# Attention issued as a listed order of small steps on three engines, and two moves in the rounds of an S5 stage

## The chip, the cores and the metric

The kernel runs on one core of a Trainium2 chip. The metric is the device time of that core in microseconds, as the median of several runs. Before the change it is 1025.93 us, the median of 3 runs from 1025.42 to 1026.64. Engines are named as the profile names them: PE is TensorE (matrix products and transposes, with PEld for its weight loads), DVE is VectorE, ACT is ScalarE, POOL is GpSimd, and SP is the engine that issues the large transfers.

## What is computed

A decoder trunk of two layers over one sequence of 256 tokens with 1024 channels in float32. Each layer is half a SwiGLU block, a mixer, and half a SwiGLU block again. Layer 0 mixes with S5, a diagonal state-space recurrence; behind it one set of keys and values is made. Layer 1 mixes with attention of three branches (compressed, selected, window) over that set. Cut to what matters here:

```python
def _swiglu(x, w_in, w_out):                 # D_FF 2816
    a, b = jnp.split(x @ w_in, 2, axis=-1)
    return (jax.nn.silu(a) * b) @ w_out

def _s5_mixer(u, ..., w_glu):                # 64 groups of 16 channels, 64 states
    bu_re = jnp.einsum('bsgh,gph->bsgp', ug, bb_re)      # and bu_im
    _, _, x_re, x_im = lax.associative_scan(combine, (la_re, la_im, bu_re, bu_im), axis=1)
    y = einsum(x_re, c_re) - einsum(x_im, c_im) + d_skip * ug
    y = jax.nn.gelu(y.reshape(bsz, seq, D_MODEL))
    return y * jax.nn.sigmoid(y @ w_glu)

def _nsa_mixer(u, kv, w_qg, q_norm, w_o, rel_bias):      # 16 heads in 4 groups, head size 64
    qg = u @ w_qg
    q = _rmsnorm(qg[..., :1024].reshape(bsz, seq, 4, 4, 64), q_norm)
    gates = jax.nn.sigmoid(qg[..., 1024:].reshape(bsz, seq, 4, 4, 3))
    o = gates[..., 0:1] * o_cmp + gates[..., 1:2] * o_slc + gates[..., 2:3] * o_win
    return o.reshape(bsz, seq, D_MODEL) @ w_o

for layer in range(2):
    h = h + 0.5 * _swiglu(_rmsnorm(h, ffn1_norm[layer]), ...)
    h = h + mixer(_rmsnorm(h, mix_norm[layer]))
    h = h + 0.5 * _swiglu(_rmsnorm(h, ffn2_norm[layer]), ...)
```

## The kernel before

**Products and weights.** A float32 product is made of three products of a shorter type. Each operand is split into a high part and a remainder, and `mm3` (lines 139 to 141) adds high times high, remainder times high and high times remainder in one bank. Weights come as raw blocks of 1 MB over SP's queue into two buffers. ACT copies the high part (`whi`, lines 92, 105, 131) and DVE subtracts it for the remainder (`wlo`, lines 96, 108, 132); there are five buffers for each. The left operand, the normalised activations `xT`, is made by PE transposes (line 180) that ACT and DVE empty in the same two parts (lines 188 and 189, or 164 and 165). An object `Acts` does that for one half of a token tile at a time (`fill`). After the first of tile 1 has been filled it also issues the squares of all rows (line 156, ACT) and the reciprocal root of their means (`rs`, lines 160 and 161, DVE and POOL).

**The blocks.** A SwiGLU block takes its weights from a generator of split blocks and multiplies chunk after chunk. At its end it hands each finished half of a token tile to `done`, which fills the operand of what follows. PE has no gap between the blocks if that operand and the first split weights are there.

**S5** works in eight rounds `cb` of 8 groups. PE makes the drive of the states (`dr`, line 542), DVE rotates it (`turn_in`, line 522), scans (line 559) and rotates back (`turn_out`, with POOL adding up `z`, line 566), and PE makes the outputs (`yb`, lines 573 and 580), which ACT passes through the gelu. The GLU product of the round before (`ga`, lines 139 to 141) lies between, and each round also splits the weights of the round three later (`weights`, lines 92 and 96). Here DVE, ACT and PE run in the order in which the program is written (`manual_schedule`), so the order of the calls in the loop is the order in each engine's queue. Ahead of the rounds stand 15 products whose result nothing reads (line 612). A round in short, with the two neighbours that matter below:

```python
turn_out(cb)
if cb + 3 < KT:
    weights(cb + 3)          # high part on ACT, remainder on DVE
outputs(cb)
if cb + 1 < KT:
    turn_in(cb + 1, dr)
```

**Attention** is cut into about 35 units in a string `ORD`: `q` makes the queries of one of four head groups ("chunks") for both token tiles, `t` transposes them, `l` makes the logits and exponentials of one group and one token tile, `c` the compressed branch of a group, `m` scales the exponentials, transposes them and multiplies by the values, `p` adds a part of the final projection. The string gives priorities to the compiler's scheduler, which orders the single instructions of neighbouring units on each engine. In `queries` the two token tiles go together: both are scaled (`qs`, line 875) and squared (line 878) by ACT, one DVE call sums the squares of both, POOL raises them to the power -1/2 (`hrr`, line 715), one DVE call multiplies (line 885), and the two are split and transposed (line 894) into `qT`. The first chunk is 304 columns wide, since it also has the gates (line 877); the others have 256. Logits (`s`, line 930) go to two banks, with two more (`x`) for the window part of token tile 1; DVE adds the bias and finds the maximum (lines 936 and 938), ACT takes the exponential (line 941). The projection's last part adds to `h` and calls `done`, which fills the operand of the last SwiGLU block.

Engines take their queues strictly in order, and an instruction that waits holds all behind it.

## Time and profile before

| | us | PE busy us | granted clock |
|---|---|---|---|
| median of 3 runs | 1025.93 | | |
| profiled execution | 1024.85 | | |
| its span, first to last instruction | 1023.1 | 984.84 | 0.988 |
| 0 to 219: first SwiGLU block | 219.00 | 209.56 | 1.00 |
| 219 to 330: most of S5 | 111.00 | 104.29 | 0.92 |
| 330 to 711.7: end of S5, two SwiGLU blocks, keys and values | 381.70 | 378.73 | 1.00 |
| 711.7 to 833.4: attention | 121.70 | 106.59 | 0.97 |
| 833.4 to 1023: last SwiGLU block | 189.60 | 185.67 | 1.00 |

The span is the time from the first to the last instruction of one profiled execution. Times within it count from its first instruction. The granted clock is the share of PE's full speed that it was allowed; a matrix product takes twice as long at 0.50. A stage in which PE is busy for its whole length at clock 1.00 can only become shorter if PE gets less to do.

### The profile page before, as it was taken

What the parts mean: (1) busy time and instruction counts of PE and PEld (TensorE: products, weight loads), DVE (VectorE), ACT (ScalarE), POOL (GpSimd) and SP (SyncE); (2) the same over time, 40 slices, a digit from 0 to 9 for tenths busy, and PEclk for the clock granted to TensorE, in tenths of its full rate; (3) what the DMA queues carried; (4) which work ended last, traced back from release to release, by engine and by line L of the source; (5) the groups of instructions that cost most, each with busy time, mean ns of one, the idle gap of its engine ahead of it and who ended that gap; (6) DMA issues with size and microseconds to landing.
All of it is one profiled execution on the core that took longest, in us unless ns stands there. A gap on an engine that the chain in (4) does not pass through costs nothing.

```text
span 1023.1 us, 14326 instructions
## 1 busy us (share of the span) xinstructions
PE 984.8 (96%) x5532; PEld 802.5 (78%) x5532; DVE 658.8 (64%) x1194; ACT 578.9 (57%) x1015; POOL 80.1 (8%) x88
## 2 busy tenths in 40 slices
PE   6999999989999999999999999999798899999998
PEld 5888887778778877888878888888676678888886
DVE  4999954479765455567565555556588866655553
ACT  5677675544465345456655555554687665555552
POOL 3001120313110000000032000000200000000000
PEclk9999999979999999999999999999899999999999
DMA  7556564443157657664645455553511145555642
GB/s 264 184 191 212 196 206 130 159 121 109 63 175 206 181 164 202 210 225 149 248 160 201 132 202 174 197 185 106 170 31 54 42 148 195 193 190 181 204 171 78
DMA packets 28948, 168.96 MB, mean 165 GB/s; under 512 B 4560, under 2 KB 7184, under 8 KB 10064
## 3 DMA queue, kind: packets, MB, share of 16 engines
q1 hardware_dynamic: 28656, 167.26, 49.0%
q8 instruction: 43, 0.70, 0.3%
q0 software_dynamic: 224, 0.79, 0.2%
q14 instruction: 25, 0.20, 0.1%
HBM read 165.54 MB, written 2.49 MB: 164 GB/s over the span
## 4 chain that ended last, share of the span: by engine, by line
PE 88%; DVE 4%; ACT 4%; POOL 1%; issue 1%; DMA 0%; SPq 0%; ACTq 0%; POOLq 0%
PE mm L139 17%; PE mm L140 16%; PE mm L141 16%; PE o L140 8%; PE o L141 8%; PE o L139 8%; PE tr L226 2%; PE dr L542 1%; PE x L969 1%; PE tr L959 1%; PE ga L141 1%; PE tr L797 1%; ACT Pt L941 1%; PE tr L180 1%; PE ga L139 1%
## 5 line engine op out<-in xcount | busy, mean ns | idle before, releaser
L139 PE MATMUL mm<-whi,xT 128*128 128x512 f32 (+2 forms) x800 | 313.9, 394 | 9.8 <-ACT qst L878 4.0
L141 PE MATMUL mm<-whi,xT 128*128 128x512 f32 (+2 forms) x800 | 307.3, 385 | 1.4 <-DVE xT L189 1.4
L140 PE MATMUL mm<-wlo,xT 128*128 128x512 f32 (+2 forms) x800 | 307.5, 385 | 0.6 <-DVE wlo L96 0.5
L108 DVE SCALAR_TENSOR_TENSOR wlo<-raw,gains,whi 128x512 fp32r<-128x512 f32 x288 | 203.6, 748 | 94.1 <-ACT whi L105 90.9
L105 ACT ACTIVATE whi<-raw,gains 128x512 fp32r<-128x512 f32 x288 | 192.1, 718 | 115.1 <-PE mm L141 51.1
L96 DVE TENSOR_TENSOR wlo<-raw,whi 128x1024 fp32r<-128x1024 f32 x148 | 182.1, 1236 | 109.6 <-ACT whi L92 109.2
L92 ACT ACTIVATE whi<-raw 128x1024 fp32r<-128x1024 f32 x148 | 155.0, 1059 | 123.9 <-PE mm L141 48.4
L139 PEld LDWEIGHTS mm<-whi,xT 128*128 128x128 f32 x800 | 151.9, 190 | 41.1 <-ACT qst L878 4.5
L141 PEld LDWEIGHTS mm<-whi,xT 128*128 128x128 f32 x800 | 151.6, 190 | 31.5 <-DVE xT L189 1.9
L140 PEld LDWEIGHTS mm<-wlo,xT 128*128 128x128 f32 x800 | 152.3, 190 | 28.4 <-DVE wlo L96 1.5
L140 PE MATMUL o<-wlo,turned 128*128 128x512 f32 x352 | 137.8, 391 | 0.1
L141 PE MATMUL o<-whi,turned 128*128 128x512 f32 x352 | 137.5, 391 | 0.0
L139 PE MATMUL o<-whi,turned 128*128 128x512 f32 x352 | 137.1, 392 | 0.0
L140 PEld LDWEIGHTS o<-wlo,turned 128*128 128x128 f32 x352 | 66.1, 188 | 14.3 <-DVE wlo L96 1.0
L141 PEld LDWEIGHTS o<-whi,turned 128*128 128x128 f32 x352 | 66.2, 188 | 13.6
L139 PEld LDWEIGHTS o<-whi,turned 128*128 128x128 f32 x352 | 66.0, 188 | 13.8 <-ACT g L265 0.3
L265 ACT ACTIVATE g<-mm,rs 128x256 f32<-128x256 f32 x88 | 41.0, 471 | 44.5 <-PE mm L141 44.0
L266 DVE SCALAR_TENSOR_TENSOR g<-mm,rs,g 128x256 f32<-128x256 f32 x88 | 41.8, 482 | 36.9 <-ACT g L265 36.8
L165 DVE TENSOR_TENSOR turned<-tr,turned 128x512 fp32r<-128x512 f32 x44 | 30.3, 689 | 31.9 <-ACT turned L164 31.6
L164 ACT ACTIVATE turned<-tr 128x512 fp32r<-128x512 f32 x44 | 26.2, 595 | 38.7 <-PE tr L226 38.6
L941 ACT ACTIVATE Pt<-Pt,mx 128x128 f32<-128x128 f32 (+1 forms) x64 | 28.4, 447 | 4.4 <-DVE mx L936 4.3
L161 POOL TENSOR_TENSOR rs<-ms,nhalf 128x1 f32<-128x1 f32 x12 | 6.6, 554 | 302.3 <-DVE ms L160 302.3
(298 smaller groups left out, 941.4 us busy)
## 6 DMA issues: line engine op xcount, KB each, us to landing
raw<-in_w_in_dram SPq DMA_DIRECT2D x87, 1024.0 KB, 4.9
raw<-in_w_out_dram SPq DMA_DIRECT2D x44, 1024.0 KB, 4.9
raw<-in_w_kv_dram SPq DMA_DIRECT2D x6, 1024.0 KB, 4.8
raw<-in_w_glu_dram SPq DMA_DIRECT2D x4, 1024.0 KB, 4.9
raw<-in_w_o_dram SPq DMA_DIRECT2D x4, 1024.0 KB, 4.9
raw<-in_w_qg_dram SPq DMA_DIRECT2D x6, 512.0 KB, 3.6
B<-revd SPq DMA_DIRECT2D x8, 256.0 KB, 7.9
raw<-in_w_qg_dram SPq DMA_DIRECT2D x2, 608.0 KB, 3.8
```

The source lines that it names most:

```text
L92: Last.act = S.activation(hi, r, AF.Copy)
L96: Last.dve = V.tensor_tensor(out=lo, in0=r, in1=hi.bitcast(F32), op=ALU.subtract)
L105: Last.act = S.activation(hi[:, c], r[:, c], AF.Identity, scale=g_)
L108: i = V.scalar_tensor_tensor(out=lo[:, c], in0=r[:, c], scalar=g_, in1=hi[:, c].bitcast(F32), op0=ALU.mult, op1=ALU.subtract)
L139: T.matmul(ps, lhsT=xh, rhs=wh, start=start, stop=False)
L140: T.matmul(ps, lhsT=xh, rhs=wl, start=False, stop=False)
L141: Last.pe = T.matmul(ps, lhsT=xl, rhs=wh, start=False, stop=stop_)
L164: i = S.activation(dst_hi, src, AF.Copy)
L165: V.tensor_tensor(out=dst_lo, in0=src, in1=dst_hi.bitcast(F32), op=ALU.subtract)
L265: Last.act = S.activation(sl, acc[t][:, 0:256], AF.Silu, scale=rs[:, t:t + 1])
L266: Last.dve = V.scalar_tensor_tensor(out=g[:, t, :], in0=acc[t][:, 256:512], scalar=rs[:, t:t + 1], in1=sl, op0=ALU.mult, op1=ALU.mult)
L941: S.activation(Pt[:, r, br], Pt[:, r, br], AF.Exp, scale=-1.0, bias=mx[:, c:c + 1], accum_out=sm[:, c:c + 1])
```

## The change

The change has three parts.

1. **Attention.** `ORD` and its units are replaced by `ORDER`, a list of 397 names, and the scheduler is switched off for PE, ACT and DVE, so that the list is the order in each queue. A name is a letter with numbers: `h w` split the query weights, `g` makes six products of a query chunk for one token tile, `a b n i j y x` are the norm, split and transposes of one chunk and one token tile, `l v e` the logits, bias and exponential of one head, `c C k K q z Z` the compressed branch, `s S` the scaling, `t T P` the transposes, their copies and the product with the values, `o O` the split of the output, `D H W M` the weights and products of the projection, `A B Y U` the addition to `h` and the operand of the last block. The norm of the queries is now by token tile, each with its own squares, sums, power and multiply. The norm factor and the operand of token tile 1 are made in attention (`f F J Q R`), while tile 0's are made at the end of the block before (`fill_half`). `E` is an exponential of one element whose result nothing reads. `L N V` load and split the first weights of the last SwiGLU block (the class `Ahead`).
2. **S5, round zero.** Ten products whose result nothing reads are issued ahead of `turn_out(0)`.
3. **S5, all rounds.** `weights` is cut in two: the high part stays where it was, the remainder on DVE goes behind `turn_in(cb + 1)`.

The code, cut; the steps that are left out hold the old units' instructions, one or two to a step:

```diff
+        def norm(self):
+            for u in range(4):
+                row_square(self.h, u // 2, u % 2, self.ss)
+            for u in range(2):
+                row_rstd(u, self.ss, self.rs)
+
+        def fill(self, t, kq, norm=True):
+            pv = self.turn(t, kq)
...
+            if norm and t + kq == 2:
...
+    class Ahead:
...
+        def load(self):
+            n = len(self.raws)
+            self.raws.append(load_granule(self.w_in[n // 2, n % 2], 512))
+
...
+            def weights(k, part):
+
+                r = raws[k // 2][:, (k % 2) * 1024:(k % 2 + 1) * 1024]
+                if part == 0:
+                    hi, lo = hip.tile([P, 1024], F32R, name="whi"), lop.tile([P, 1024], F32R, name="wlo")
+                    S.activation(hi, r, AF.Copy)
+                    gw[k] = [(hi[:, n * 512:(n + 1) * 512], lo[:, n * 512:(n + 1) * 512]) for n in range(2)]
+                    rooms[k] = hi, lo
+                    return
+                hi, lo = rooms.pop(k)
+                V.tensor_tensor(out=lo, in0=r, in1=hi.bitcast(F32), op=ALU.subtract)
                 if k in (2, 3):
                     raws.append(load_granule(A["w_glu"][k], 512))
+
...
+            def spin(ps, n):
+
+                for i in range(n):
+                    T.matmul(ps, lhsT=gw[0][0][0][:, 0:P], rhs=gw[0][0][0], start=True, stop=True)
...
+                    if cb == 0:
+                        spin(gacc[1][1], 10)
                     turn_out(cb)
                     if cb + 3 < KT:
-                        weights(cb + 3)
+                        weights(cb + 3, 0)
                     outputs(cb)
                     if cb + 1 < KT:
                         turn_in(cb + 1, dr)
+                    if cb + 3 < KT:
+                        weights(cb + 3, 1)
                 for t in range(2):
                     yk[t, 0] = y_tokens(t, 0, pd, "dr")
...
-    ORD = "q0 q1 t0 l00 l01 q2 t1 c0 m00 l10 m01 l11 q3 t2 c1 m10 l20 m11 l21 t3 c2 m20 l30 m21 l31 c3 p0 p2 m30 p4 m31 p6"
...
+    ORDER = """
+    Q0 f0 d10 g000 F00 f1 g001 J00 d11 F01 h100 F10 J01 w100 d20 F11 g010 J10 g002 h110 J11 Q1 g011 g003 g012 R g013 a00 w110 b00
+    a01 d21 g110 b01 h200 n00 g111 w200 g100 g112 g101 E i00 j00 g113 h210 y00 x00 g102 n01 d30 w210 l000 i01 j01 l001 a11 v000 y01
...
+    def attention(x, hc, ahead):
...
+            def step_g(n, t, i):
+                if i == 0:
+                    qa[n, t] = mm_bank()
+                w = width(n)
+                for k in (2 * i, 2 * i + 1):
+                    u = (n, k // 4, 0 if n else k % 4 // 2)
+                    c = (k % 4 if n else k % 2) * w
+                    mm3(qa[n, t][:, 0:w], xT, k, t, (wh[u][:, c:c + w], wl[u][:, c:c + w]), k == 0, k == KT - 1)
...
+            def step_a(n, t):
+                q, v = tp.tile([P, 256], F32, name="qs"), tp.tile([P, 4, 2, 64], F32R, name="qst")
+                qq[n, t], qv[n, t] = q, v
+                    S.activation(rsh[:, t:t + 1], rs[:, t:t + 1], AF.Copy, scale=0.5)
+                S.activation(v.rearrange("p h a d -> p (h a d)")[:, 0:256].bitcast(F32), qa[n, t][:, 0:256], AF.Square, scale=rs[:, t:t + 1])
+                S.activation(q, qa[n, t][:, 0:256], AF.Identity, scale=rs[:, t:t + 1])
+                if n == 0:
+                    S.activation(gate[:, t].rearrange("p h b -> p (h b)"), qa[n, t][:, 256:304], AF.Tanh, scale=rsh[:, t:t + 1])
+
+            def step_E():
+                S.activation(small.tile([P, 1], F32, name="warm"), rsh[:, 1:2], AF.Exp)
+
+            def step_b(n, t):
+                ss, ms = tp.tile([P, 4], F32, name="hss"), tp.tile([P, 4], F32, name="hms")
+                sq = qv[n, t].rearrange("p h a d -> p (h a d)")[:, 0:256].bitcast(F32)
+                V.tensor_reduce(out=ss, in_=sq.rearrange("p (h d) -> p h d", d=64), axis=mybir.AxisListType.X, op=ALU.add)
+                V.tensor_scalar(out=ms, in0=ss, scalar1=1.0, scalar2=64 * EPS, op0=ALU.mult, op1=ALU.add)
+                rr = tp.tile([P, 4], F32, name="hrr")
+                G.tensor_tensor(out=rr, in0=ms, in1=nhalf[:, 0:4], op=ALU.pow)
+                qp[n, t] = rr
...
+            def step_n(n, t):
+                q3 = qq[n, t].rearrange("p (h d) -> p h d", d=64)
+                V.tensor_tensor(out=q3, in0=q3, in1=qp[n, t].unsqueeze(2).to_broadcast([P, 4, 64]), op=ALU.mult)
...
+            def step_l(g, t, r):
+                ps = s_bank()
+                parts = [(ps[:, 0:400], 0, 400)] if t == 0 else [(ps[:, 0:KWN], 0, KWN), (x_bank()[:, 0:256], KWN, KW)]
+                for i in range(2):
+                    for p_, c0, c1 in parts:
+                        T.matmul(p_, lhsT=qT[:, g * 4 + r, t * P:(t + 1) * P], rhs=KV.kT[:, i, g, c0:c1], start=i == 0, stop=i == 1)
+                lb[g, t, r] = ps, ps[:, KWN:400] if t == 0 else parts[1][0]
...
+            def step_T(g, t, kb, br):
+                pts[g, t, kb, br] = pt_room[:, turn[0] % 4]
+                turn[0] += 1
+                if br:
+                    V.tensor_copy(pts[g, t, kb, br], tp_[g, t, kb, br])
+                else:
+                    S.activation(pts[g, t, kb, br], tp_[g, t, kb, br], AF.Copy)
...
+            steps = {k[5:]: f for k, f in locals().items() if k.startswith("step_")}
+            for kh in range(2):
+                step_d(0, kh)
+                for j in range(2):
+                    step_h(0, kh, j)
+                    step_w(0, kh, j)
+            with tc.manual_schedule(engines={V.engine, S.engine, T.engine}):
+                for u in ORDER.split():
+                    steps[u[0]](*(int(i) for i in u[1:]))
+            Nxt.x.norm()
...
+    def fill_half(hc, gain):
+
+        def done(t, hf):
+            if t == 0 and hf == 0:
+                acts(hc, gain)
+            if t == 0:
+                Nxt.x.fill(0, hf, norm=False)
+                row_square(hc, 0, hf, Nxt.x.ss)
+                if hf:
+                    row_rstd(0, Nxt.x.ss, Nxt.x.rs)
         return done
...
-        ffn(x, 3, A["w_in1_1"], A["w_out1_1"], h, bg=bg, steps=1, done=fill_next(h, 4))
-    attention(Nxt.x, h, fill_next(h))
+        ffn(x, in_granules(A["w_in1_1"], 3), A["w_out1_1"], h, bg=bg, steps=1, done=fill_half(h, 4))
+    ahead = Ahead(A["w_in2_1"], 5)
+    attention(Nxt.x, h, ahead)
...
-    ffn(Nxt.x, 5, A["w_in2_1"], A["w_out2_1"], h, done=store)
+    ffn(Nxt.x, ahead, A["w_out2_1"], h, done=store)
```

How this moves instructions is shown at three places, one row for each instruction in an engine's queue: line, operation, what is written and what is read, size; numbers behind a name tell buffers apart.

The first place is ACT's queue where the first query products end, before the change (`h` is squared into `ss`, `mm` are the query banks, `qst` holds the queries' squares and later their split, `whi` are high parts of weights):

```order
L156 ACTIVATE junk_6156,ss_6082<-h_75 128x512
L156 ACTIVATE junk_6158,ss_6082<-h_75 128x512
L156 ACTIVATE junk_6160,ss_6082<-h_75 128x512
L875 ACTIVATE qs_6268<-mm_6198,rs_6081 128x256
L156 ACTIVATE junk_6162,ss_6082<-h_75 128x512
L131 ACTIVATE whi_6493<-raw_6491 128x1024
L877 ACTIVATE gate_6193<-mm_6198,rsh_6188 128x48
L878 ACTIVATE qst_6269<-mm_6198,rs_6081 128x256
L875 ACTIVATE qs_6268<-mm_6199,rs_6081 128x256
L877 ACTIVATE gate_6193<-mm_6199,rsh_6188 128x48
L878 ACTIVATE qst_6269<-mm_6199,rs_6081 128x256
```

Four squares of rows for both token tiles, one of them and a weight split within the evacuations of the two banks, stand here. The same place after the change, from the first evacuation on:

```order
L1003 ACTIVATE qst_6292<-mm_6205,rs_6091 128x256
L1004 ACTIVATE qs_6291<-mm_6205,rs_6091 128x256
L1006 ACTIVATE gate_6169<-mm_6205,rsh_6165 128x48
L1002 ACTIVATE rsh_6165<-rs_6091 128x1
L1003 ACTIVATE qst_6306<-mm_6243,rs_6091 128x256
L1004 ACTIVATE qs_6305<-mm_6243,rs_6091 128x256
L1006 ACTIVATE gate_6169<-mm_6243,rsh_6165 128x48
L967 ACTIVATE whi_6326<-raw_6239 128x1024
L1009 ACT_TABLE_LOAD
L1009 ACTIVATE warm_6356<-rsh_6165 128x1
L1025 ACTIVATE qst_6292<-qs_6291 128x4x64
```

Each token tile's three evacuations stand together now, the square ahead of the copy. The squares of `h` have moved ahead of them or into the block before, one weight split lies behind both tiles, and the table of the exponential is loaded before the queries' first split.

The second place is PE's queue at the first logits. Before, from the last products of the second query chunk (`tr` are transposes of the queries, `s` the logits):

```order
L139 MATMUL mm_6287<-whi_6320,xT_6080 128x256
L140 MATMUL mm_6287<-wlo_6321,xT_6080 128x256
L141 MATMUL mm_6287<-whi_6320,xT_6080 128x256
L894 MATMUL tr_6363<-ident_76,qst_6269 128x128 x4
L894 MATMUL tr_6369<-ident_76,qst_6269 128x128 x4
L930 MATMUL s_6380<-kT_4271,qT_6190 128x400 x2
L930 MATMUL s_6388<-kT_4271,qT_6190 128x400 x2
L139 MATMUL mm_6459<-whi_6463,xT_6080 128x256
L140 MATMUL mm_6459<-wlo_6464,xT_6080 128x256
L141 MATMUL mm_6459<-whi_6463,xT_6080 128x256
```

Both tiles' transposes stand ahead of the first logits. After the change:

```order
L126 MATMUL mm_6337<-whi_6258,xT_6090 128x256
L127 MATMUL mm_6337<-wlo_6297,xT_6090 128x256
L128 MATMUL mm_6337<-whi_6258,xT_6090 128x256
L1048 MATMUL s_6385<-kT_4281,qT_6166 128x400 x2
L1048 MATMUL s_6390<-kT_4281,qT_6166 128x400 x2
L1034 MATMUL tr_6405<-ident_76,qst_6306 128x128 x4
L1048 MATMUL s_6421<-kT_4281,qT_6166 128x400 x2
L1048 MATMUL s_6430<-kT_4281,qT_6166 128x400 x2
```

Tile 1's transposes (`qst_6306`) now stand behind the first two logits of tile 0, which directly follow a product of the second chunk (`mm_6337`).

The third place is DVE's queue between rounds zero and one of S5. Before (`z0` and `Y2` end the rotation back, `wlo` is the remainder of the weights, `X` and `Y` are the rotation into round one, the last row is its scan):

```order
L522 TENSOR_TENSOR z0_1983<-X_1979,cosT_92 128x512
L522 TENSOR_TENSOR Y2_1981<-X_1979,sinT_93 128x512
L96 TENSOR_TENSOR wlo_2068<-raw_1977,whi_2067 128x1024
L522 TENSOR_TENSOR X_1979<-dr_2053,cosT_92 128x512
L522 TENSOR_TENSOR Y_1980<-dr_2053,sinT_93 128x512
L522 TENSOR_TENSOR X_1979<-X_1979,Y_1980 128x512
L559 SCALAR_TENSOR_TENSOR X_1979<-rt_1982,X_1979 128x512
```

After:

```order
L572 TENSOR_TENSOR z0_1983<-X_1979,cosT_92 128x512
L572 TENSOR_TENSOR Y2_1981<-X_1979,sinT_93 128x512
L572 TENSOR_TENSOR X_1979<-dr_2053,cosT_92 128x512
L572 TENSOR_TENSOR Y_1980<-dr_2053,sinT_93 128x512
L572 TENSOR_TENSOR X_1979<-X_1979,Y_1980 128x512
L552 TENSOR_TENSOR wlo_2078<-raw_1977,whi_2077 128x1024
L609 SCALAR_TENSOR_TENSOR X_1979<-rt_1982,X_1979 128x512
```

The remainder moved behind the three calls of the rotation, ahead of the scan; the same in each later round that has one.

More of the change, by code (lines that the diff above doesn't have):

```diff
@@ L216, in ffn @@
             acc2 = [[pa.tile([P, 512], F32, name=f"o{t}{hf}") for hf in range(2)] for t in range(2)]
-            g_in = granules([w_in[c, kh] for c in range(NCH) for kh in range(2)], gain=gi, first=first)
             g_out = granules([w_out[j] for j in range(NCH)])
@@ new lines, in attention, with room, width, part @@
+            acc = []
+            raw, wh, wl, qa, qv, qq, qp, lb, Pt, mx, sm, cl, tp_, pts, ob, fp = ({} for _ in range(16))
+            def room(pool, name, c):
+                return pool.tile([P, 1024], F32R, name=name)[:, 0:c]
+            def width(n):
+                return CHUNKS[n][2]
+            def part(n, kh, j):
+                c = 4 * width(n) // (1 if n else 2)
+                return raw[n, kh][:, j * c:(j + 1) * c]
+            def step_d(n, kh):
+                raw[n, kh] = load_granule(A[f"w_qg{n}"][kh], width(n))
```

363 lines of the change are left out of this document (201 added, 162 removed).

## The prediction, made before the changed kernel was run

> **What bounds the kernel now.** I read the page first: the busy times, then the 40 slices.
>
> ```profile
> PE 984.8 (96%) x5532; PEld 802.5 (78%) x5532; DVE 658.8 (64%) x1194; ACT 578.9 (57%) x1015; POOL 80.1 (8%) x88
> ...
> PE   6999999989999999999999999999798899999998
> ...
> PEclk9999999979999999999999999999899999999999
> ```
>
> TensorE (PE) is busy 96% of the span, so an edit pays only where PE is idle or its clock is low. The slices (25.6 us each) show two such places behind the start: slice 9, where the S5 stage begins (8 tenths, clock 7), and slices 29 to 32, attention (down to 7 tenths, clock 8 in slice 29). Those are the stages that the change touches. Next I cut attention into stages. In the second fence the columns are: stage in us, its length, busy time (and instructions) of PE, PEld, DVE (VectorE), ACT (ScalarE) and POOL (GpSimd), granted clock, DMA share, GB/s.
>
> ```profile
> 711.70:736.30 24.60, 18.34 (x114) 16.43 (x112) 14.92 (x28) 16.22 (x37) 3.82 (x3) 0.86 0.48 151
> 736.30:833.40 97.10, 88.25 (x548) 65.60 (x549) 77.78 (x324) 66.81 (x199) 5.17 (x5) 1.00 0.19 66
> ```
>
> At 711.7 the first query product starts, at 736.3 the first logits, at 833.4 the first product of the last feed-forward block. The opening wastes 6.3 of 24.6 us of PE, and runs at clock 0.86. The long stage has PE at 88.25 of 97.10 and DVE at 77.78: no engine is full, so waits set it. Who waits in the opening is in the timeline (start, duration, engine, line, operation, and in brackets the idle time before it):
>
> ```profile
> 725.13 1.04 ACT L131 ACTIVATE whi<-raw 128x1024 fp32r<-128x1024 f32 x1
> 726.50 0.47 ACT L878 ACTIVATE qst<-mm,rs 128x256 f32<-128x256 f32 x1
> 727.01 0.58 PE L139 MATMUL mm<-whi,xT 128*128 128x256 f32 x1 [3.37 <-ACT qst L878]
> 731.62 0.69 DVE L885 TENSOR_TENSOR qs<-qs,hrr 128x512 f32<-128x512 f32 x1 [1.54 <-POOL hrr L715]
> 736.29 0.97 PE L930 MATMUL s<-kT,qT 128*128 128x400 f32 x4 [0.30 <-issue]
> 737.43 1.28 ACT L941 ACT_TABLE_LOAD   x1
> ```
>
> PE stands 3.37 us because ACT, between four row squares and a weight split, is late in emptying the query banks. Only at 731.62 are the norms of both token tiles there.
>
> **Attention, the opening.** The change takes the two tiles apart: tile 0's norm chain runs while PE multiplies tile 1. PE's list ahead of the first logits is 48 products of 304 columns, 42 of 256 and three groups of four transposes. Their pitches come from neighbours in the timeline:
>
> ```profile
> 714.54 0.30 PE L141 MATMUL mm<-whi,xT 128*128 128x304 f32 x1
> 714.68 0.30 PE L139 MATMUL mm<-whi,xT 128*128 128x304 f32 x1
> ...
> 732.20 0.28 PE L140 MATMUL mm<-wlo,xT 128*128 128x256 f32 x1
> 732.32 0.28 PE L141 MATMUL mm<-whi,xT 128*128 128x256 f32 x1
> ...
> 734.96 1.03 PE L894 MATMUL tr<-ident,qst 128*128 128x128 f32 x8
> ```
>
> 48 x 0.14 + 42 x 0.12 + about 1.3 for twelve transposes is 13.1 us. ACT has more to do. Of its 16.22 us in the old opening, two weight splits (2 x 1.04), the second chunk's first evacuations (0.9) and one transposed-query evacuation (0.6) now come after the first logits, and the narrower split saves 0.3; the exponential's table load (1.28, and 0.2 for a warming call) and two 0.2 us scalings come ahead of them. That is 14.8 us. If ACT has no holes, the first logits come at 711.7 + 14.8 = **726.5 instead of 736.3**. Of these 9.8 us, 6.3 are idle time and about 2.4 the half speed from 727.0 to 731.8 (the clock rows below); PE waits some 1.7 itself. Six products and four transposes that used to lie ahead of the first logits now follow them: 1.2 us that PE still has to do.
>
> **Attention, the rest.** PE's work from the first logits on is bounded by its 88.25 us of busy time; with the 1.2 it is 89.5. DVE's 77.78 grow: three weight splits that used to lie in the opening move behind the first logits (3 x 1.22, the row at 239.03 below), and norms by tile are two half-size calls for one. The row at 731.62 has 0.69 for 512 columns, the next fence 0.42 for 256, so each of three calls costs 0.15 more and each scaling call 0.17; about 0.6 per chunk, 1.9 for three chunks. DVE has 83.4 us.
>
> ```profile
> L165 DVE TENSOR_TENSOR oT<-x,oT 128x256 fp32r<-128x256 f32 x6 | 2.5, 423 | 0.8 <-ACT oT L164 0.8
> ```
>
> The waits of the long stage (us in total, times, longest) come next:
>
> ```profile
> PE s L930 <- DVE clg L938: 3.6, 3, 1.3
> PE tr L914 <- DVE pst L165: 3.4, 2, 2.7
> ...
> DVE qs L885 <- POOL hrr L715: 4.5, 3, 1.6
> ```
>
> They say what an order can win: 7.0 us of PE stand behind VectorE's results, and 4.5 us of DVE behind GpSimd's power, because the multiply directly follows it in DVE's queue. The listed order puts other DVE work between the two. Nothing in the trace shows the new order, so I bound it. The quick end is PE without a hole: 89.5 us, end at 816.0. The slow end keeps every hole of before and adds DVE's 5.6 us: 102.7, end at 829.2. I take the middle, 96.1, because about half of the long waits listed have a remedy in the list while the queues stay strictly ordered. The feed-forward block's first product then starts at 822.6 instead of 833.4: **-10.8 us**, between -17.4 and -4.2. PE is full right behind that point before (the stage 833.4 to 860 has no PE idle time), and the new list has the same two transposes and products there, with three weight splits made ahead.
>
> **S5, rounds zero and one.** The next fence is the timeline of DVE, POOL and PE.
>
> ```profile
> 223.11 0.68 DVE L522 TENSOR_TENSOR Y<-X,sinT 128x512 f32<-128x512 f32 x1
> 223.88 1.26 POOL L566 TENSOR_TENSOR z<-z,Y 128x512 f32<-128x512 f32 x1 [8.27 <-DVE Y L522]
> 224.10 2.12 DVE L96 TENSOR_TENSOR wlo<-raw,whi 128x1024 fp32r<-128x1024 f32 x1 [0.31 <-ACT whi L92]
> 226.14 0.68 DVE L522 TENSOR_TENSOR X<-dr,cosT 128x512 f32<-128x512 f32 x1
> 227.04 3.68 PE L542 MATMUL dr<-turned,WBT 128*128 128x64 f32 x16
> 231.47 0.63 PE L141 MATMUL ga<-whi,xT 128*128 128x512 f32 x1
> 231.90 0.63 PE L139 MATMUL ga<-whi,xT 128*128 128x512 f32 x1
> 233.28 0.68 DVE L522 TENSOR_TENSOR X<-dr,cosT 128x512 f32<-128x512 f32 x1
> 234.77 0.65 PE L573 MATMUL yb<-turned,Wi 128*32 128x64 f32 x32
> 236.24 2.00 PE L542 MATMUL dr<-turned,WBT 128*128 128x64 f32 x16
> 239.03 1.22 DVE L96 TENSOR_TENSOR wlo<-raw,whi 128x1024 fp32r<-128x1024 f32 x1
> ```
>
> The weight remainder (L96, 2.12 beside POOL's 1.26, 1.22 later) stands ahead of the rotation into the next round (X<-dr). Moved behind it, it lets the rotation start at 223.8 instead of 226.14, and again at 230.8 instead of 233.28. Behind the moved call waits only the scan, and that would wait for the rotation anyway. PE must follow, and its clock decides that:
>
> ```profile
> 216.39:219.80 3.41, 2.61 (x24) 2.64 (x24) 2.14 (x5) 1.48 (x2) 0.00 (x0) 1.00 0.83 209
> ...
> 223.21:226.63 3.42, 1.44 (x56) 1.44 (x60) 3.11 (x3) 0.86 (x1) 1.26 (x1) 0.50 0.03 7
> 226.63:230.04 3.41, 3.41 (x34) 3.24 (x27) 3.34 (x6) 1.65 (x4) 0.00 (x0) 0.50 0.80 271
> 230.04:233.45 3.41, 3.41 (x11) 2.83 (x11) 3.29 (x4) 0.97 (x2) 1.27 (x1) 0.50 0.84 344
> 233.45:236.87 3.42, 3.42 (x108) 2.81 (x107) 3.02 (x4) 0.49 (x1) 0.00 (x0) 1.00 0.02 5
> ...
> 721.56:724.97 3.41, 1.16 (x5) 0.49 (x3) 1.65 (x3) 3.24 (x10) 0.56 (x1) 1.00 0.49 178
> 724.97:728.39 3.42, 1.38 (x6) 1.38 (x7) 2.19 (x5) 3.30 (x9) 0.56 (x1) 0.50 0.22 89
> 728.39:731.80 3.41, 3.41 (x18) 3.41 (x17) 1.78 (x4) 0.43 (x1) 2.71 (x1) 0.50 0.74 195
> 793.24:796.65 3.41, 1.55 (x12) 1.51 (x13) 3.32 (x24) 2.23 (x9) 0.00 (x0) 1.00 0.00 0
> ```
>
> I chose stages of 3.41 us because the clock changes only on that grid. It is half from 219.80 to 233.45, and comes back after a stage full of 512-column products. The ten idle products start where the old round's first small products did, about 221.8. At the half-clock pitch of 0.43 (rows 231.47 and 231.90) they last to 226.1, and fill the stage 223.21 to 226.63, where PE was busy 1.44. If full speed is back at 226.6, round zero's outputs end about 228.0 (0.9 later than now), the next drive needs 2.0 instead of 3.68, the GLU's twelve products 2.8 instead of 5.1, and round one's outputs start at 232.7 instead of 234.77: **-2.1 us**. The later rounds are full on PE, and carry it on. The other end is a clock that the spin does not lift: the 0.9 and the half-speed GLU make +2.9. I take -2.1, since the row 230.04:233.45, also all 512-column products, was followed by full clock.
>
> The Trainium skill ("TensorE: Matmul & The Clock Gate", Part 1) says that the clock falls after an idle window of about 3.4 us and returns after a busy one. By this rule the spin works, or one window later, which would leave -0.7. The trace agrees on the return, but not on the fall: the stage 216.39:219.80 was busy 2.61 of 3.41 and was still followed by half clock.
>
> **Sum.** -10.8 - 2.1 = -12.9. The profiled execution took 1024.85 us around its span of 1023.1, so 1012.0; the median of the runs, 1025.93, lies 1.1 above that execution, so **1013 us** is forecast, and the other times below count from the median too. Outside these two stages PE's list is as before.
>
> **Rivals.**
> (a) *The order packs no better.* The slow end of attention with the S5 gain: -4.2 - 2.1, 1019.6 us. For it: DVE's load rises from 77.8 to 83.4, and DVE is a second engine near full. Against: the 4.5 us behind POOL have a remedy.
> (b) *The order packs fully.* -17.4 - 2.1, 1006.4 us. Against: three queues in strict order never fit exactly.
> (c) *The clock falls in the new lean stretch, or the spin does not lift it.* Between the last query products and the first projection, PE has only logits, transposes and small products, while DVE is full. Each stage at half clock delays by at most 1.7; three of them make 5.1, a failed spin 5.0 against the forecast: about 1018. Against: the stage 793.24:796.65 was busy only 1.55, and stayed at 1.00. For: 1.16 did not suffice at 721.56.
> The Trainium skill speaks for (c): the same page, Part 4, has transposes not counting as busy for the clock. By it the lean stretch would be throttled, again about 1018; the stage 793.24:796.65 does not bear it out.
> (d) *Slower: PE blocked on the logits banks.* There are two of them; each logits step in PE's queue waits until DVE has read the bank before last, and the query products and transposes queued behind it cannot pass. The longest such wait is 1.3 us (three times in 3.6 now). The list has 32 logits steps, and puts DVE's splits, scalings and copies between the reads. From 10 uncovered waits of 1.3 on (13 us) the forecast's gain is gone; with every second step waiting, 16 x 1.3 = 20.8, the kernel takes 1013 + 20.8 = 1034. Against: the first query products lie between the steps as filler.
>
> **How the numbers follow.** Forecast 0.52, (a) 0.15, (b) 0.11, (c) 0.10, (d) 0.09, and 0.03 for the two gains eaten up to nothing measurable. About 0.2%, 2 us, is what a measurement can tell from no change. The forecast, (a), (b) and (c) are all faster by more: 0.88; slower is (d), 0.09; within it 0.03. The range from 1004 to 1021 takes in both ends of the attention bound with S5 at -2.1 and leaves out (d), and (a) together with a failed spin.
>
> **What would show it.** Right: first logits (L1048) by 727, less S5's 2.1; no half clock between 715 and 735; DVE's wait for POOL near nothing; the last feed-forward block's first product near 820; clock 1.00 from about 226.6 and round one's outputs at 232.7. Wrong: ACT with holes in the opening, DVE under 81% busy behind it, PE rows that wait for clg or Pt of DVE, or clock rows of 0.50 in attention.

## The result, and the profile after

| | before | after |
|---|---|---|
| median of 4 runs, us | 1025.68 (1024.96 to 1026.64) | 1009.03 (1006.76 to 1010.04) |
| ratio, 95% interval | | 0.9834 (0.9815 to 0.9853) |
| profiled execution, us | 1024.85 | 1010.04 |

The kernel became 16.7 us faster; 12.9 were forecast. The profiled execution of the changed kernel, 14.8 us under that of before, is the slowest of its four runs; the one execution of 2499.7 us, of the variant below without the early loads, is left out of that variant's ratio. Its page, busy times and slices:

```profile
PE 977.5 (97%) x5542; PEld 800.8 (79%) x5542; DVE 656.3 (65%) x1209; ACT 577.4 (57%) x1022; POOL 79.7 (8%) x92
...
PE   6999999999899999999999999999998999999998
...
PEclk9999999989999999999999999999999999999999
```

The dip of PE in attention is down to one slice of 8 tenths, and the clock of 7 in slice 9 is 8. To place the gain I cut both traces at the same instructions: the last addition to `h` ahead of S5, S5's last transposes of `h`, the first addition at the end of the block behind it, the second group of transposes of `h` at the end of the block before attention (709.38 before, 707.65 after; called T0 below), the first logits, and the last block's first product. The windows of before, then of the changed kernel, with the columns of the prediction's windows:

```profile
213.28:289.63 76.35, 69.95 (x1059) 58.17 (x1058) 63.27 (x91) 30.85 (x51) 17.16 (x18) 0.89 0.32 102
289.63:471.21 181.58, 178.35 (x800) 145.08 (x800) 102.33 (x142) 95.82 (x149) 1.10 (x2) 1.00 0.64 194
471.21:709.38 238.17, 236.84 (x1117) 195.47 (x1115) 141.60 (x213) 132.16 (x204) 20.27 (x27) 1.00 0.52 179
...
709.38:736.29 26.91, 20.65 (x125) 18.43 (x125) 16.70 (x33) 18.05 (x41) 3.82 (x3) 0.87 0.44 138
736.29:833.42 97.13, 88.28 (x549) 65.63 (x549) 77.80 (x324) 66.84 (x199) 5.17 (x5) 1.00 0.19 66
```

```profile
213.36:286.82 73.46, 68.52 (x1069) 56.82 (x1068) 61.15 (x91) 30.66 (x51) 14.89 (x18) 0.95 0.32 106
286.82:469.46 182.64, 178.70 (x800) 145.00 (x800) 102.08 (x142) 96.14 (x149) 1.10 (x2) 1.00 0.64 193
469.46:707.65 238.19, 236.86 (x1118) 195.40 (x1116) 141.49 (x213) 132.75 (x206) 20.26 (x27) 1.00 0.52 179
...
707.65:725.66 18.01, 16.15 (x115) 14.92 (x115) 13.47 (x32) 15.26 (x39) 4.29 (x4) 1.00 0.36 108
725.66:818.63 92.97, 86.74 (x559) 69.49 (x559) 80.23 (x340) 68.97 (x210) 7.12 (x9) 0.98 0.23 78
```

S5 gave 2.9 us (2.1 forecast), the opening of attention 8.9 (9.8), its long stage 4.2 (1.0). The stretch between S5 and T0, whose instructions are almost the same, took 1.1 us more; the last section says why. The last block takes 189.7 us in both.

The timeline of the changed kernel in S5:

```profile
222.40 4.18 PE L662 MATMUL ga<-whi 128*128 128x512 f32 x10
225.91 1.22 DVE L552 TENSOR_TENSOR wlo<-raw,whi 128x1024 fp32r<-128x1024 f32 x1
232.72 0.65 PE L623 MATMUL yb<-turned,Wi 128*32 128x64 f32 x32
```

The ten products last to 226.6, the clock is back at 225.9, the remainder follows the rotation, and round one's outputs start at 232.72, where 232.7 was forecast. The timeline at the start of attention shows a hole that no term of the prediction had:

```profile
711.89 0.66 PE L167 MATMUL tr<-ident,h 128*128 128x128 f32 x4 [1.74 <-DVE xT L178]
712.30 0.38 PE L126 MATMUL mm<-whi,xT 128*128 128x304 f32 x1
```

The listed order has token tile 1's transposes ahead of the first query product, and they wait for a bank that DVE still reads. ACT had holes too: these are its waits between T0 and the first logits (in total, times, longest; the second began ahead of T0).

```profile
ACT xT L180 <- DVE xT L178: 1.3, 3, 0.7
ACT junk L143 <- DVE xT L178: 0.9, 1, 0.9
ACT rsh L1002 <- POOL rs L148: 0.8, 1, 0.8
ACT qT L1038 <- PE tr L1034: 0.3, 1, 0.3
```

The waits of PE in the long stage (first two rows) and of DVE from T0 on (the rest):

```profile
PE s L1048 <- DVE clg L1065: 2.7, 4, 1.6
PE tr L1099 <- DVE pst L1093: 1.5, 2, 1.2
```

```profile
DVE turned L1127 <- PE tr L1120: 4.0, 3, 2.0
DVE h L1177 <- PE x L128: 3.2, 2, 2.5
DVE oT L1154 <- ACT oT L1150: 2.4, 2, 1.2
```

DVE's 4.5 us behind POOL's power are gone: no such row is left. The two rows of PE come to 4.2 us, where the two of before came to 7.0; two waits of PE for DVE's `oT`, of 0.9 and 0.5 us, are new.

### The profile page after: what moved, and what is told of

The parts are those of the page before. It is cut to its first block, busy times and chain, and to the rows that moved or that the text cites. A ratio compares the mean times of both kernels' runs of the same rounds, so it can differ in the third digit from the quotient of the medians.

```text
span 1008.3 us, 14376 instructions
## 1 busy us (share of the span) xinstructions
PE 977.5 (97%) x5542; PEld 800.8 (79%) x5542; DVE 656.3 (65%) x1209; ACT 577.4 (57%) x1022; POOL 79.7 (8%) x92
## 4 chain that ended last, share of the span: by engine, by line
PE 86%; DVE 7%; ACT 4%; DMA 1%; issue 1%; POOL 1%; SPq 0%; ACTq 0%; POOLq 0%
PE mm L126 16%; PE mm L127 16%; PE mm L128 16%; PE o L128 8%; PE o L127 8%; PE o L126 8%; PE tr L265 2%; PE dr L592 1%; DVE Pt L1063 1%; DMA raw<-in_w_in_dram 1%; PE tr L855 1%; DVE wlo L96 1%; PE tr L167 1%; PE ga L128 1%; PE tr L1120 1%
## 5 line engine op out<-in xcount | busy, mean ns | idle before, releaser
L108 DVE SCALAR_TENSOR_TENSOR wlo<-raw,gains,whi 128x512 fp32r<-128x512 f32 x282 | 198.8, 748 | 91.7 <-ACT whi L105 89.1
L105 ACT ACTIVATE whi<-raw,gains 128x512 fp32r<-128x512 f32 x282 | 188.0, 718 | 111.6 <-PE mm L128 51.7
L96 DVE TENSOR_TENSOR wlo<-raw,whi 128x1024 fp32r<-128x1024 f32 x132 | 160.6, 1224 | 105.1 <-ACT whi L92 104.8
L92 ACT ACTIVATE whi<-raw 128x1024 fp32r<-128x1024 f32 x132 | 138.1, 1059 | 120.4 <-PE mm L128 46.9
L127 PEld LDWEIGHTS o<-wlo,turned 128*128 128x128 f32 x352 | 66.1, 188 | 14.3 <-DVE wlo L96 1.0
```

The lines of the kernel that those rows point to most:

```text
L92: Last.act = S.activation(hi, r, AF.Copy)
L96: Last.dve = V.tensor_tensor(out=lo, in0=r, in1=hi.bitcast(F32), op=ALU.subtract)
L105: Last.act = S.activation(hi[:, c], r[:, c], AF.Identity, scale=g_)
L108: i = V.scalar_tensor_tensor(out=lo[:, c], in0=r[:, c], scalar=g_, in1=hi[:, c].bitcast(F32), op0=ALU.mult, op1=ALU.subtract)
L127: T.matmul(ps, lhsT=xh, rhs=wl, start=False, stop=False)
```

## The experiments

In the first four the parts are taken apart. Ratios are to the kernel before, on the same chip, with 95% intervals. Stages are read from T0 (the second transposes of `h`) where it matters, because all that lies ahead of T0 varies from execution to execution.

**Only the ten products**

```diff
+                    if cb == 0:
+                        for i in range(10):
+                            T.matmul(gacc[1][1], lhsT=gw[0][0][0][:, 0:P], rhs=gw[0][0][0], start=True, stop=True)
                     turn_out(cb)
```

> The kernel before with only the ten idle products ahead of turn_out(0). Theory P (the products lift the clock, and the clock is what S5 loses by): half speed from about 219 to 226 only, round one's outputs near 233, and about -1.5 to -2.5 us of the kernel before; the weight remainder is still ahead of the rotation, so DVE is up to 0.5 us late for round one. Rival Q (both edits are needed, because the rotation comes late): the clock rises, PE then waits for DVE, and the time stays within 0.5 us of the kernel before.

Measured: 0.998 (0.9968 to 0.9991), about -2.1 us. In its profiled execution the clock was not halved in S5 at all, so this trace shows the rounds at full speed with the old place of the remainder. Its windows and PE's waits:

```profile
212.68:287.58 74.90, 66.45 (x1069) 53.98 (x1068) 63.27 (x91) 30.98 (x51) 17.75 (x18) 1.00 0.32 104
```

```profile
PE yb L580 <- POOL z L566: 2.7, 3, 1.3
PE ga L141 <- DVE xT L522: 2.4, 4, 1.0
```

Even at full clock S5 takes 74.9 us and not the changed kernel's 73.5: PE now waits for DVE and POOL.

**Only the remainder moved**

```diff
                     if cb + 3 < KT:
-                        weights(cb + 3)
+                        weights(cb + 3, 0)
                     outputs(cb)
                     if cb + 1 < KT:
                         turn_in(cb + 1, dr)
+                    if cb + 3 < KT:
+                        weights(cb + 3, 1)
```

> The kernel before with only the weight remainder moved behind the rotation. Theory P: the clock is still half until about 233.4, PE is full from 226.6 on and sets the pace, so the rotation is 2.1 us earlier and the time within 0.3 us of the kernel before. Rival Q (the order on DVE is what counts): round one's outputs near 233 and -1.5 us or more.

Measured: 1.0007 (0.9991 to 1.0023), no change that can be told. Its window:

```profile
213.20:289.66 76.46, 68.49 (x1060) 56.95 (x1059) 61.13 (x91) 30.72 (x51) 14.89 (x18) 0.91 0.31 101
```

S5 takes 76.46 us against 76.35 before. As theory P has it, the earlier rotation alone is worth nothing.

**Both edits in S5**: the two diffs above together, with the old attention.

> The kernel before with both edits in S5 and the old attention. Prediction's term: -2.1 us. By the profile of the changed kernel the end of S5 comes 2.8 us earlier, of which 1.06 are lost at a weight block that lands late about 100 us later: between -1.7 and -2.8 us. Rival: the lead is lost wholly to that load and the time stays within 0.3 us.

Measured: 0.9967 (0.9953 to 0.998), -3.4 us. Its window and PE's waits:

```profile
213.66:287.12 73.46, 68.51 (x1070) 56.88 (x1069) 61.13 (x91) 30.64 (x51) 15.35 (x18) 0.95 0.33 106
```

```profile
PE yb L591 <- POOL z L577: 0.8, 1, 0.8
PE ga L141 <- DVE xT L533: 0.7, 2, 0.4
```

The two waits of the first run fall from 5.1 to 1.5 us, and S5 takes 73.46 us, the same as in the changed kernel. The products bring the clock: at the start of S5 it was at half for 13.7, 10.2 and 13.7 us in the three profiled executions without them (before, only the remainder, only attention), and in the ten with them for 6.8 us in seven and not at all in three. The moved remainder is worth something only once they have. By profile the pair shortens S5 by 2.9 us, the products alone by 1.45, and the remainder alone lengthens it by 0.1; by times the difference between the pair and the sum (3.4 against 1.4) lies within the intervals. The plainest pair of traces has the clock at 1.00 in the whole of S5: 74.90 us with the products alone, 71.93 and 71.85 with both, in two runs below (the first query products ahead, and the old order of units). At full clock the moved remainder is worth 3.0 us.

**Only attention**: the changed kernel with the S5 rounds of before (both diffs above undone).

> The changed kernel with S5 as it was before (no ten products, remainder ahead of the rotation). Theory P (the two gains add): attention is worth -13.1 us by the two profiles (from the last transposes of the block before, 707.65 against 709.38, to the first product of the last block, 818.63 against 833.42), so 1012.6 us on a median of 1025.7. Prediction's own term: -10.8 us. Rival (part of the attention gain rests on S5's, by where the clock's windows fall): -15 us or more, or less than -11.

Measured: 0.9861 (0.9844 to 0.9879), -14.3 us. From T0 to the last block it takes 110.77 us (709.87 to 820.64), against 110.98 in the changed kernel and 124.04 before. The two gains add: 14.3 + 3.4 = 17.7 beside 16.7 measured for both, within the intervals.

**Tile 0's squares back in attention.** It tests whether ACT sets the opening.

```diff
             if t == 0:
                 Nxt.x.fill(0, hf, norm=False)
-                row_square(hc, 0, hf, Nxt.x.ss)
-                if hf:
-                    row_rstd(0, Nxt.x.ss, Nxt.x.rs)
...
+            def step_1(hf):
+                row_square(hc, 0, hf, x.ss)
...
+            def step_2():
+                row_rstd(0, x.ss, rs)
```

In the list, `10` stands behind `F10`, `11` ahead of `Q1`, and `2` ahead of `R`.

> The changed kernel with the squares and the norm factor of token tile 0 back in attention, among the query weights' splits as before, instead of in the end of the block before. It adds two squares of 0.82 us each to ACT in the opening. Theory P (ACT sets the opening, as the prediction had it): first logits 1.6 us later, about 15 us behind the first query product instead of 13.36, and 1 to 1.6 us slower in all. Rival (PE sets it; it is busy 13.24 of the 13.36 us, and ACT has room): 0.4 us or less.

Measured: 0.9824 (0.9797 to 0.9852). First logits 19.39 us behind T0 instead of 18.01, later as theory P has it, by 1.4 us and not 1.6. From T0 to the last block's first product it is 111.56 against 110.98; the rest came back in the long stage (92.17 instead of 92.97, at clock 1.00 instead of 0.98), and the times cannot tell it from the changed kernel, where 1 to 1.6 us more were expected.

**The first query products ahead of tile 1's transposes.** It is meant to remove PE's hole.

```diff
-    Q0 f0 d10 g000 F00 f1 g001 J00 d11 F01 h100 F10 J01 w100 d20 F11 g010 J10 g002 h110 J11 Q1 g011 g003 g012
+    Q0 g000 d10 f0 F00 g001 f1 J00 d11 F01 h100 F10 J01 w100 d20 F11 g002 J10 g010 h110 J11 Q1 g011 g003 g012
```

> The changed kernel (fixed order) with the first four query products' steps moved ahead of the transposes of token tile 1, so that PE's hole of 1.74 us at the start of attention goes. Theory P (ACT's list sets the opening): the first query product comes 1.7 us or more earlier, but the first logits still 18.0 us behind the last block's second transposes, and the time stays within 0.5 us of the changed kernel. Rival (PE sets the opening, being busy 13.24 of its 13.36 us): first logits 0.8 to 1.7 us earlier, and the time with them.

Measured: 0.9815 (0.9793 to 0.9836). The first query product came 2.3 us behind T0 (703.97 to 706.31) instead of 4.65, and the first logits 18.21 instead of 18.01. The opening is as long as before, although PE starts 2.3 us sooner. These are PE's waits in it:

```profile
PE tr L167 <- DVE xT L178: 0.9, 1, 0.9
PE mm L126 <- ACT gate L1007: 0.7, 2, 0.5
```

About half of the hole is still there, now behind the first six products, and PE also waits for ACT to empty a query bank. ACT's own waits are the four of the changed kernel, of the same length. So the start of PE's products is not what sets the opening. Both runs speak for ACT's list, together with its waits for DVE and POOL; a shorter DVE list was not tried.

**The multiply directly behind POOL's power.** Each `n` step of the list moved behind its `b` step, eight times, as here for the first chunk:

```diff
-    a00 w110 b00 a01 d21 g110 b01 h200 n00 g111 w200 g100 g112 g101 E i00 j00 g113 h210 y00 x00 g102 n01 d30
+    a00 w110 b00 n00 a01 d21 g110 b01 n01 h200 g111 w200 g100 g112 g101 E i00 j00 g113 h210 y00 x00 g102 d30
```

> The changed kernel with each multiply by the norm directly behind the power on POOL that it needs, on DVE's queue (eight of them), as the kernel before had three. Theory P (the distance between them is one of the remedies): DVE waits for POOL about 1 us in each of the eight, 6 to 9 us in all; those of the chunks in the stretch where DVE is full (740 to 777 us) count, so 3 to 5 us slower than the changed kernel. Rival (the waits lie where DVE has room, or the moved multiply only frees later work): under 1 us.

Measured: 0.9915 (0.9887 to 0.9943), 1018.3 us. Its windows from T0 on, and the waits of DVE and PE:

```profile
706.93:726.01 19.08, 16.18 (x115) 14.91 (x115) 13.53 (x32) 15.39 (x39) 4.11 (x4) 1.00 0.33 89
726.01:826.31 100.30, 88.03 (x558) 69.75 (x559) 80.58 (x339) 68.94 (x210) 7.00 (x9) 0.98 0.22 74
```

```profile
DVE qs L1023 <- POOL hrr L1018: 8.2, 7, 1.2
```

```profile
PE s L1049 <- DVE clg L1066: 7.6, 7, 3.2
```

DVE's waits for POOL are back, 8.2 us, and the way from T0 to the last block grew by 8.4 (119.38 against 110.98). It is worse than the 3 to 5 us expected: in the sum the waits pass on nearly one for one. PE's wait for the logits banks went from 2.7 to 7.6 us.

**Three remainders of w_o later.** `W10`, `W11` and `D3` (the load of the fourth block of w_o) left their places in the list for one behind `M00`, and `W20` for one behind `M10`. The rows are cut to the parts that differ:

```diff
-    v313 D3 l213 t2000 l300 v213 M00 l301 e213
+    v313 l213 t2000 l300 v213 M00 W10 W11 D3 l301 e213
...
-    M10 e302 q2 W21
+    M10 W20 e302 q2 W21
```

> The changed kernel with three remainders of w_o (1.22 us each on DVE, at 764.7, 766.5 and 771.0) moved behind the projection's first steps, where PE is full, and the load of the fourth w_o block behind them. Theory D (DVE is the bound from 743 to 777 us: it is busy 2.7 to 3.0 of each 3 us while PE is at 1.4 to 3.0): 2 to 3.7 us faster than the changed kernel. Rival E (ACT, busy 2.4 to 3.0 in most of these slices, or the order of PE's queue is the bound as well): under 0.7 us either way.

Measured: 0.9824 (0.9794 to 0.9853), not to be told from the changed kernel. The long stage took 91.25 us at clock 1.00; the two runs above with clock 1.00 there (squares back, first query products ahead) took 92.17 and 92.21. So about 1 us by one execution of each, between the two expectations. DVE is nearly full in the changed kernel's stretch ahead of the projection:

```profile
743.66:776.66 33.00, 27.42 (x188) 20.06 (x187) 32.32 (x147) 26.91 (x91) 3.13 (x5) 0.98 0.19 65
```

It is busy 32.32 of 33 us, but taking 3.7 us off it gives only 1, so DVE is not the only bound there.

**Without the early loads and splits of the last block's weights**

```diff
-    A11 B11 Y11 Y10 U11 U10 V2
+    A11 B11 Y11 Y10 U11 U10
...
-    ffn(Nxt.x, ahead, A["w_out2_1"], h, done=store)
+    ffn(Nxt.x, in_granules(A["w_in2_1"], 5), A["w_out2_1"], h, done=store)
```

The other `L`, `N` and `V` steps go as well.

> The changed kernel (fixed order) without the early loads and splits of the last block's weights: the block makes them itself, behind attention's list. Theory P (the prediction took the entry as hidden only because of them): loads can still start when a buffer comes free, but the splits come behind the last operand pieces on ACT and DVE, so PE waits 1.5 to 4 us at the first product of the last block. Rival (the load is late as well): 5 to 8 us. Rival (ACT and DVE have room enough at the end): under 0.5 us.

Measured: 0.982 (0.9797 to 0.9843), not to be told from the changed kernel. Only its times are used. They show no loss, but with intervals of about 2.4 us to either side they do not exclude the lower end of the 1.5 to 4 us that theory P expected. So the theory that the entry is hidden by these splits has no support here, and PE's wait at the entry was not seen.

**The list without the fixed order**

```diff
-            with tc.manual_schedule(engines={V.engine, S.engine, T.engine}):
-                for u in ORDER.split():
-                    steps[u[0]](*(int(i) for i in u[1:]))
+            for u in ORDER.split():
+                steps[u[0]](*(int(i) for i in u[1:]))
```

> The changed kernel with the same steps in the same list, but without the fixed order: the scheduler orders the instructions on PE, ACT and DVE as in the kernel before. Theory L (the listed order is worth what the long stage gained, the norms by tile what the opening gained): first logits still about 13.5 us behind the first query product, the long stage (first logits to the last block's first product) back near 97 us instead of 92.97, the kernel 3 to 6 us slower than the changed one. Rival M (the small steps and norms by tile carry the whole gain): within 1.5 us of the changed kernel. Rival N (the fixed order carries it all): within 3 us of the kernel before.

Measured: 0.9781 (0.9755 to 0.9807), 1004.4 us, faster than the changed kernel. Its windows from T0 on, and PE's waits in the long stage:

```profile
706.72:724.73 18.01, 16.90 (x115) 15.14 (x115) 13.15 (x34) 15.35 (x40) 3.14 (x4) 1.00 0.39 118
724.73:814.63 89.90, 86.42 (x554) 68.22 (x555) 77.95 (x338) 68.07 (x208) 7.00 (x9) 0.98 0.23 78
```

```profile
PE tr L1120 <- ACT qT L1038: 1.7, 2, 1.5
PE x L126 <- DVE mx L1063: 0.5, 1, 0.5
PE tr L1034 <- DVE turned L1127: 0.4, 1, 0.4
```

The opening is as long, 18.01 us; the long stage is 89.90 instead of 92.97. No row of PE waiting for the logits banks is left; PE is idle for 3.5 us instead of 6.2. Theory L fell: the order in the list, used as priorities, gains more than the same order forced on the queues.

**The new steps in the old order of units.** The list is rewritten so that all steps of a unit stand together (all query products of a chunk, then its norms, its transposes, a whole logits unit, and so on as in the old string), and the scheduler orders the engines.

```diff
-    Q0 f0 d10 g000 F00 f1 g001 J00 d11 F01 h100 F10 J01 w100 d20 F11 g010 J10 g002 h110 J11 Q1 g011 g003 g012 R g013 a00 w110 b00
+    f0 F00 F01 J00 J01 f1 F10 F11 J10 J11 Q0 Q1 R g000 g001 g002 g003 g010 g011 g012 g013 a00 a01 G b00 b01 n00 n01 i00 i01 j00 j01
...
+    l000 v000 e000 l001 v001 e001 l002 v002 e002 l003 v003 e003 l010 v010 e010 l011 v011 e011 l012 v012 e012 l013 v013 e013
```

Its fixed order is taken off as in the run before, and `E` is not in it, so the exponential's table is loaded behind the first logits (1.28 us on ACT, at 727.05) and not ahead of them.

> The changed kernel's small steps, norms by token tile and early weights, but listed unit by unit as the old string has its units (each unit's steps together), and ordered by the scheduler. Theory S (the small steps and norms by tile carry the gain, the scheduler finds the order): within 3 us of the run without the fixed order (1004.4), so 1003 to 1008. Rival L (the interleaved list carries it, as priorities or as order): 1015 or more. In between: both.

Measured: 0.9919 (0.9896 to 0.9942), 1018.0 us. Its windows from T0 on:

```profile
705.03:725.19 20.16, 17.52 (x126) 16.09 (x125) 14.47 (x35) 14.92 (x39) 3.25 (x4) 1.00 0.34 105
725.19:825.17 99.98, 91.85 (x544) 67.57 (x545) 79.78 (x338) 70.03 (x208) 6.85 (x9) 0.97 0.23 80
```

The opening has most of the gain (20.16 us against 26.91 before and 18.01), the long stage none: 99.98 against 97.13 before. So the steps and norms by tile carry most of the opening (which is here without the table load), and the interleaved list carries the long stage, from 99.98 to 89.90 with the scheduler and to 92.97 with the fixed order.

**The list without the fixed order, and the three remainders later**: the two edits together, with the same list as in the run with the remainders later.

> The run without the fixed order, with the three remainders of w_o later in the list. In the fixed order that shortened the stretch from the last block's second transposes to the next block's first product from 110.98 to 109.38 us. Theory D (DVE is still the bound before the projection): 0.5 to 1.6 us faster than without the move (1004.4), about 1003.3. Rival (the stage is at PE's floor, 89.9 us against 88 us busy): within 0.5 us.

Measured: 0.9804 (0.9784 to 0.9825), 1005.6 us. From T0 to the last block 107.44 us (708.39 to 815.83) against 107.91 without the move. The times do not tell the two apart; both beat the changed kernel in this stage by about 3 us.

## Why the prediction was right, step by step

**The opening: right in place and in cause, in size by two errors that nearly cancel.** The forecast was 14.8 us of ACT's list from the first query product, without holes. The terms as the prediction lists them add up to 14.2; 14.8 comes out if the 0.6 for a transposed-query evacuation is not taken off, and rightly so, since one such evacuation lies ahead of the first logits both before (735.60) and after (724.96). A term is missing: the two squares of token tile 0, of 0.82 us each, which the change takes out of the opening. So ACT had less to do than forecast: from T0 on it was busy 15.26 us instead of 18.05. But the forecast put its holes at nothing, and ACT stood idle for 2.7 of the 18.01 us; holes of ACT were one of the prediction's own signs of being wrong. From T0 on the gain was 8.9 us where 9.8 were forecast, and that it came so close is partly luck. From the first query product it took 13.36 us, but that product came 4.65 us behind T0 instead of 2.32: 1.74 us of this are PE's hole, which no term had. That ACT's list sets the opening was tried from both sides: two squares more on ACT made the first logits 1.4 us later, an earlier start of PE gave nothing, and both speak for it. The half clock that stood at 725 to 732 before is gone.

**The long stage: the mechanism was right, the term mis-sized.** The forecast took the middle between 89.5 and 102.7, 96.1; it was 92.97. Three parts of that term were too large. DVE's load was to grow by 5.6 us; its busy time grew by 2.4, from 77.80 to 80.23. By DVE's groups the three query splits (3.7 us) and the halved calls of the norms (2.1 more) are there as forecast, and two splits of the last block (1.5 us) fell behind the stage. The rest is that the forecast added up the calls' own times. Those grew by 4.8 us, from 100.3 to 105.2; they add up to more than the stage, since neighbouring calls overlap in the trace, and the busy time counts an overlap once. The waits of DVE for POOL, for which the forecast took half the remedies to work, are all gone; putting them back cost the stage and the opening 8.4 us for 8.2 us of waiting. And the quick end, 89.5, was no floor: it rests on PE's busy time of before and 1.2 us more, but PE's busy time in the stage fell, from 88.28 to 86.74.

**S5: right to 0.1 us at the point that was worked out.** Round one's outputs were at 232.72, 2.1 us sooner also from the last addition ahead of S5 (19.36 us instead of 21.49). In the three executions with the products in which the clock did not fall at all they came 17.8 us behind that addition with the remainder moved, and 19.0 without, so the 2.1 holds only where the clock is at half for 6.8 us. S5 as a whole gave 2.9 us, but the other 0.8 are not shown to be the change's. In the profiled execution of before the clock fell once more, late in S5:

```profile
267.57:270.98 3.41, 1.89 (x48) 1.23 (x37) 3.41 (x6) 1.56 (x3) 0.00 (x0) 1.00 0.12 48
270.98:274.40 3.42, 3.42 (x87) 2.53 (x89) 0.59 (x1) 0.00 (x0) 1.27 (x1) 0.50 0.00 0
```

From round one's outputs to the end it took 54.86 us before and 54.10 after. The run with only attention, which has the old S5 and no such fall, took 54.19. So the later rounds themselves neither gained nor lost, as the prediction had it ("The later rounds are full on PE, and carry it on"). Such a late fall is in two of the three executions without the products and in none of the ten with them; whether the products keep it away was not tried.

**Hidden entry of the last block: right, the reason not shown.** The last block took as long as before, but the three splits made ahead are not shown to be the reason: without them the times are the same within the intervals.

**The rivals.** (a), no better packing, did not come; the run that brings the waits for POOL back, at 1018.3 us, comes near its 1019.6. (b), PE without a hole, came in time but not in kind: in the run without the fixed order the stage took 89.90 us, beside the forecast's quick end of 89.5, but PE was busy for 86.42 of them. (c) came once in the changed kernel's profiled execution: the clock is at half from 775.4 to 778.8. Its price was put at up to 1.7 us; the two runs with clock 1.00 there (squares back, first query products ahead) took 92.2 us, the changed kernel 92.97, and the run with only attention 92.67 at clock 0.98. So it is about 0.6; that PE waits for DVE in that stretch anyway would explain it, but was not tried. (d), PE blocked on the logits banks, is small in the changed kernel (2.7 us), and larger in the run with the multiply behind POOL's power (7.6 us).

The rule of the Trainium skill ("TensorE: Matmul & The Clock Gate", Part 4) that stood behind (c), by which transposes don't count as busy, isn't borne out. These are two windows of the clock's grid in the changed kernel, and the one behind the second:

```profile
754.95:758.36 3.41, 2.19 (x17) 1.28 (x16) 3.27 (x20) 2.45 (x9) 0.13 (x1) 1.00 0.00 0
...
772.02:775.43 3.41, 2.21 (x12) 1.67 (x13) 3.41 (x20) 2.23 (x9) 0.00 (x0) 1.00 0.01 5
775.43:778.84 3.41, 3.41 (x17) 3.41 (x18) 3.41 (x19) 2.49 (x10) 0.00 (x0) 0.51 0.00 0
```

The first had transposes among its 2.19 us and kept its clock; the second had logits alone, 2.21 us, and lost it. If transposes counted for nothing, the first would be the emptier of the two. What decides it is open.

**What stays open.** Why the scheduler's order is 3.1 us better than the fixed one is shown only as far as PE's waits go: the 2.7 us behind the logits banks and 1.5 behind `pst` are gone, and PE's idle time falls by 2.7 us. Which moved instruction does it was not tried.

## What to carry to other kernels

Where several engines wait for each other in turns, cut the work into small steps, take independent tiles apart, and put other work between a slow helper's call and its use: the waits removed here came back as time almost one for one when they were restored. Try such a list as priorities before forcing it on the queues. When an engine has a hole, ask who sets the next hand-over: an earlier start of PE in the opening gave nothing, because ACT's list, with its waits, ended last.

## What was not expected of the hardware

The same instructions between S5 and T0 do not always take the same time. These rows are ACT's waits for weight blocks in 287 to 471 us (in total, times, longest), in the kernel before, in the changed one, and in the run with three remainders later:

```profile
ACT whi L105 <- DMA raw<-in_w_in_dram: 16.6, 8, 6.3
```

```profile
ACT whi L105 <- DMA raw<-in_w_in_dram: 18.1, 8, 7.3
```

```profile
ACT whi L105 <- DMA raw<-in_w_in_dram: 21.2, 8, 8.6
```

The stretch from S5's end to the next block's last part took 181.6, 182.6 and 185.5 us in these three (289.63 to 471.21, 286.82 to 469.46, 287.64 to 473.14). Over the 13 profiled executions used here it is the longest single wait that goes with the stretch, and not their sum. Where the longest is 4.4 to 6.3 us (six executions), the stretch takes 181.4 to 181.6; with 6.6, 6.8, 7.1, 7.3, 8.0, 8.4 and 8.6 it takes 181.9, 182.2, 182.4, 182.6, 183.3, 183.7 and 185.5. The loads of the bias table lie between those of the weights there; that they make a block late was not tried. The changed kernel's lead of 2.9 us lost 1.1 there by chance. The clock varies in the same way: for the same S5 code it was at half for 6.8 us in the changed kernel (219.1 to 225.9), and not at all in the run with the first query products ahead, whose S5 took 71.9 us instead of 73.5 (212.41 to 284.34). A profiled execution can thus be some us off the median, and stages have to be compared from a common point.
